# Two-block transformer kernel: adaptive vectors summed in PSUM during the projection, convolutions in a row, expert matrices loaded whole

## The chip, the cores and the metric

The kernel is one program on one core of a Trainium2 chip. The metric is the device time of one execution in microseconds (us). The engines are named as in the profile: PE is TensorE with its matmuls, PEld its weight loads, DVE is VectorE, ACT is ScalarE, POOL is GpSimd, SP is SyncE, which here issues nearly all loads. L180 means line 180 of the kernel before.

## What is computed

One sequence of 1024 tokens with 1024 features goes through two transformer blocks, all in fp32 (fp32 matmuls are done as three fp32r matmuls of a high and a low part). This is the reference's first block, cut to what the change touches:

```
m  = silu(c) @ w_ada + b_ada           # w_ada: 1024 x 6144, split in 6 vectors of 1024
mc = silu(c_ctx) @ w_ada + b_ada       # the same for the context's vector
hx = rms_norm(x,  g) * (1 + m[1]) + m[0]         # 1024 tokens
hc = rms_norm(ctx, g) * (1 + mc[1]) + mc[0]      # 256 tokens
q, k, v, o, gates, ga, gb = split(hx @ w_in + b_in)      # for hc too; w_in: 1024 x 2576
u  = ga * sigmoid(gb)                            # 512 channels
mixer = concat(group_norm(mlstm(q, k, v, gates)) * sigmoid(o),
               silu(layer_norm(conv31(u)))) @ w_out + b_out
x  = x + m[2] * rms_norm(mixer)
h  = rms_norm(x) * (1 + m[4]) + m[3]
x  = x + m[5] * rms_norm(moe(h))                 # 64 experts, 8 per token, and a shared one
```

The mLSTM runs in both directions in chunks of 128 tokens, the two chunks of the context first. `conv31` is a depthwise convolution of width 31 along rows of 64 tokens. Each expert has three matrices of 1 MB (gate and up 1024 x 256, down 256 x 1024). The second block (attention, a state-space layer and 16 experts with the same three matrices) is changed only in the loads of its experts.

## The kernel before

Work on each engine is put in order when the program is built: a list scheduler takes the instructions in program order as priority, plays them on a timeline with estimated costs, and emits one sequence per engine. The exceptions are stretches written out by hand: SP's loads in the input norm (L298 to L306) and in the main loops over the experts. An engine runs its sequence strictly in order. A tile from a pool waits for the last readers of the tile whose room it takes, and so does the load into it.

**Adaptive vectors.** `ada_piece` (L170 to L190) makes 256 of the 6144 columns for both vectors c and c_ctx. It loads 1024 rows x 256 columns (1 MB, in runs of 1 KB) and does eight fp32 matmuls, one for each 128 rows, with `csil` (32 columns, of which two are used) as the stationary operand. The eight go in turn to four column groups of TensorE, so four partial sums stand on 4 x 32 partitions. ACT copies them to `ar` (L182), two matmuls with the selecting matrix `asel` (L187) add the four sums and turn them into a column, and DVE adds the bias into `mcol` (L188). There are 24 pieces. Pieces 0 to 7 (shift and scale of the first norm) are made in `norm_in`, where their loads alternate with those of four tiles of x; the rooms are those of the weight pools `wraw`, `whi`, `wlo`. Pieces 8 to 23 are filler in the mLSTM: `fill` (L230) makes one after each unit, again in `wraw` and `whi` buffers.

**Input norm and projection.** `norm_in` (L252) norms x and then the context: squares on ACT, transposes on PE, scale and shift to a high and a low part. `project` (L320) then makes the parts of w_in one after the other. `weight` loads 1024 x 256 columns into the one `wraw` buffer and splits them (ACT L75, DVE L76). `branch` makes u of 128 channels out of columns of two such loads, `values`, `outgate` and the `feat` loops at the end the rest. `conv` (L392) is 31 DVE operations on 128 channels x 1024 tokens (L398) and then 8 transposes, an ACT copy and a store; conv(0) to conv(2) stand in the projection, conv(3) is called in the mLSTM at unit (4, 1).

**mLSTM.** `mlstm` (L576) first transposes k in 10 steps (PSUM tile `pl`, copied by ACT, L594) and makes the products of q and k in 8 steps (PSUM tile `pi`, copied by ACT, L601), each tile with one buffer. Then come 10 x 2 units (step i, direction d), of which 16 have an output: `D` on ACT (L617) and DVE (L618), matmuls into `pi` and `pn` (L624, L627), `tm` on ACT (L632) and DVE (L633), then the state's update (L669). After it `mix_out` multiplies with w_out.

**Experts.** `weights` (L1123) loads an expert's three matrices by `halves` (L1127): two loads of 512 KB each, 4 KB a partition, into two of eight raw tiles. `split` takes each half apart, high on ACT (L83, `guh` and `wdh`) and low on DVE (L84). Room for `raw` is moved between pools by hand in the set-up (`moe.room`, with Z = 3 extra tiles early on).

Of the kernel before, what the change touches and what calls it, by code (L numbers as in the profile page):

```python
# [29 lines left out]
class Kern:  # L30
# [126 lines left out]
    def ada_setup(self, pool, psp):  # L157
# [7 lines left out]
        self.asel = self.keep.tile([128, 2], F32, name="asel")  # L165
        nc.vector.reduce_sum(self.asel, self.ident.rearrange("p (w q) -> p q w", w=4)[:, 0:2], axis=AX.X)
# [36 lines left out]
    def mixer(self, es0, sec):  # L203
# [14 lines left out]
        with ExitStack() as eh:  # L218
            hx = self.pool(eh, "hx", side="right")
            x = [hx.tile([128, 8, 1024], F32R, name=n) for n in ("hTh", "hTl")]  # L220
            self.wpools(eh, 1, 2, 2)
            psp, ptp = self.pool(eh, "prp", 5, PSUM), self.pool(eh, "prt", 2, PSUM)
            c, raw = self.norm_in(x, eh, pada, ptp, psp, v1.rearrange("p c h e -> p (c h e)"), I['w_in'][0][:, 2064:2320])
            gates, conv = self.project(raw, x, c, kT, qT, v1, gt, pada, psp, ptp, kq, cp)
        sec.bias_prep()
        with ExitStack() as es:
# [19 lines left out]
            for p in todo:  # L246
                fill(9, 1)
# [7 lines left out]
    def norm_in(self, hx, eh, pada, psp, pap, spare, first):  # L255
# [5 lines left out]
        gs = st.tile([128, 2, 8], F32, name="gs")  # L261

# [5 lines left out]
        def rows(xp, xts, g):  # L268
            n = len(xts)
            ss = st.tile([128, 4], F32, name="ss", bufs=2)  # L270
            for t, xt in enumerate(xts):
                scr = xp.tile([128, 1024], BF, name="scr", bufs=1)
                nc.scalar.activation(scr, xt, AF.Square, accum_out=ss[:, t:t + 1])
# [20 lines left out]
        with ExitStack() as es:  # L294
            xp = self.pool(es, "nix")
            xts = []
            finish = lambda: None
            with self.tc.manual_schedule(engines={mybir.EngineType.SP}):  # L298
                for i in range(8):
                    if i < 4:  # L300
                        xts.append(load(xp, I['x'][0], i, 4))
                    last, finish = finish, self.ada_piece(i, st, pap, "pf", ("wraw", "whi", "wlo", "whi", "wlo"))
                    last()
                raw = self.load_w(first)
                xts += [load(spare, I['x'][0], t, 0) for t in range(4, 8)]
            finish()  # L306
            rows(xp, xts[:4], 0)
# [3 lines left out]
            rows(xp, xts[4:], 1)  # L311
# [3 lines left out]
        with ExitStack() as es:  # L315
            xp = self.pool(es, "nic")
            xts = [load(xp, I['ctx'][0], t, 2) for t in range(2)]
            rows(xp, xts, 2)
            columns(xts, 1, hc, 0)
        ew.close()  # L320
        return hc, raw

    def project(self, raw, hx, hc, kT, qT, v1, gt, pada, psp, ptp, kq, cp):
        nc, I = self.nc, self.I
        W, B = I['w_in'][0], I['b_in'][0]
        with ExitStack() as es:
            bp = self.pool(es, "prb")
            self.pcol = self.columns(bp, pada, "pcol", [B[0:512], B[1552:2576], I['conv_b'][0], I['conv_ln_g'][0], I['conv_ln_b'][0],
                                                        I['mlstm_norm_g'][0].rearrange("h p -> (h p)")])
# [48 lines left out]
            us = {}  # L378

            def branch(cc, wb, wa):  # L380
# [4 lines left out]
                for i, s in enumerate(TT):  # L385
                    pb = feat(wb, (cc % 2) * 128, hx, s)
                    sg = cp.tile([128, 512], F32, name="sg", bufs=1)
                    nc.scalar.activation(sg, pb, AF.Sigmoid, bias=bcol[:, 8 + cc:9 + cc])
                    pa = feat(wa, (cc % 2) * 128, hx, s)
# [3 lines left out]
            def conv(cc):  # L393
                u = us[cc]
                y = cp.tile([128, 16, 64], F32, name="y", bufs=1)
# [3 lines left out]
                yf = y.rearrange("p r t -> p (r t)")  # L399
# [28 lines left out]
            wb, wa = self.split_w(raw), self.weight(W[:, 1552:1808])  # L428
            branch(0, wb, wa)
            branch(1, wb, wa)  # L430
# [1758 lines left out]
Z = 3  # L2189
# [72 lines left out]
```

## Time and profile before

| what | value |
|---|---|
| runs, median (lowest to highest) | 2698.14 us (2696.0 to 2704.96), 3 runs |
| profiled execution, its own time | 2692.12 us |
| its span in the profile | 2690.3 us |
| mean granted clock of TensorE | 0.963 |
| busy: PE, PEld, DVE, ACT, POOL | 93%, 79%, 67%, 50%, 20% |
| DMA | 507.52 MB in 259820 packets, mean 189 GB/s |
| queue 1 (SP's loads) | 409.36 MB, 45.4% of 16 engines' span |
| queue 0 (gathers and scatters) | 90.98 MB, 14.9% |

The span is a little shorter than the execution's own time, since that counts what lies around the recorded instructions. Busy shares are means over stages that differ much: start, projection, mLSTM and output product, first experts (about 640 to 1541 us), second block, its experts (from about 2430 us). In a row of the timeline the columns are start, duration, engine, line, operation, output and inputs, their shapes, and the number of instructions; in square brackets stands the idle time ahead of it on its engine and what ended that.

### The profile page before, as it was taken

The numbers are of one execution on the slowest core, as the hardware profiler recorded it, in microseconds if no ns is written. First come the engines' busy times: TensorE is split into PE (matmuls) and PEld (weight loads), VectorE is DVE, ScalarE is ACT, GpSimd is POOL, SyncE is SP. The second block draws the span as 40 slices with busy tenths as digits, with TensorE's granted clock in tenths as the row PEclk, the third lists the DMA queues.
The fourth block names the chain that finished last, engine by engine and source line by source line (L and its number), as shares of the span: only waits on it lengthen the run. The fifth ranks groups of instructions, "written<-read, shape, count | busy, mean of one in ns | idle before, by whom it ended". The sixth has DMA issues, their size and how long they took to land. (4 is left out here: it accounts for less than half of the span.)

```text
span 2690.3 us, 46156 instructions
## 1 busy us (share of the span) xinstructions
PE 2492.9 (93%) x17156; PEld 2127.8 (79%) x17156; DVE 1793.0 (67%) x4037; ACT 1332.8 (50%) x2327; POOL 534.0 (20%) x467
## 2 busy tenths in 40 slices
PE   6999987999999999999999939899999989987996
PEld 4798866987988888888877628688898778976884
DVE  4874788677777788887865453763243876278882
ACT  4322156324677776767765544223222772225773
POOL 0000021311232233233233230230001200002332
PEclk9999998999999999999999969999999999997998
DMA  7111183237899999999999864444311024148995
GB/s 252 33 50 61 44 279 113 103 109 268 244 308 309 312 314 299 307 316 315 301 319 317 252 216 95 123 89 107 114 32 56 1 95 150 56 165 291 320 291 120
DMA packets 259820, 507.52 MB, mean 189 GB/s; under 512 B 68761, under 2 KB 151905, under 8 KB 259592
## 3 DMA queue, kind: packets, MB, share of 16 engines
q1 hardware_dynamic: 231720, 409.36, 45.4%
q0 software_dynamic: 26720, 90.98, 14.9%
q10 hardware_dynamic: 1152, 4.19, 0.4%
q8 instruction: 136, 2.23, 0.3%
q14 instruction: 92, 0.75, 0.1%
HBM read 414.42 MB, written 90.04 MB: 188 GB/s over the span
## 5 line engine op out<-in xcount | busy, mean ns | idle before, releaser
L84 DVE TENSOR_TENSOR gul<-raw,guh 128x1024 fp32r<-128x1024 f32 x288 | 348.4, 1219 | 114.5 <-ACT guh L83 113.4
L83 ACT ACTIVATE guh<-raw 128x1024 fp32r<-128x1024 f32 x288 | 303.1, 1061 | 176.4 <-DMA raw<-in_we_gate_dram 67.8
L1185 PE MATMUL pg<-x,guh 128*128 128x320 f32 (+8 forms) x1248 | 383.7, 371 | 2.6 <-DVE sg L1233 2.6
L1184 PE MATMUL pg<-x,gul 128*128 128x160 f32 (+8 forms) x1092 | 278.1, 256 | 0.0
L1185 PEld LDWEIGHTS pg<-x,guh 128*128 128x128 f32 x1248 | 245.2, 200 | 9.9 <-DVE sg L1233 2.7
L1269 POOL DMA_INDIRECT acc<-y,m1idx x87 | 149.3, 1717 | 492.4 <-DMA acc<-y,m1idx 103.3
L1184 PEld LDWEIGHTS pg<-x,gul 128*128 128x128 f32 x1092 | 219.0, 201 | 3.4 <-issue 0.8
L84 DVE TENSOR_TENSOR wdl<-raw,wdh 128x1024 fp32r<-128x1024 f32 x144 | 175.6, 1222 | 60.9 <-ACT wdh L83 59.3
L88 PE MATMUL psy<-wdh,hh 128*128 128x512 f32 (+8 forms) x444 | 179.2, 405 | 7.4 <-ACT y L1268 7.0
L89 PE MATMUL psy<-wdl,hh 128*128 128x512 f32 (+8 forms) x444 | 175.4, 395 | 0.0
L90 PE MATMUL psy<-wdh,hl 128*128 128x512 f32 (+8 forms) x444 | 169.5, 400 | 0.0
L1097 POOL DMA_INDIRECT xg<-h_d,m1idx x95 | 122.4, 1289 | 180.7 <-PE pt L1119 91.9
L398 DVE SCALAR_TENSOR_TENSOR y<-u,cw,y 128x1024 f32<-128x1024 f32 x120 | 153.9, 1283 | 2.7
L83 ACT ACTIVATE wdh<-raw 128x1024 fp32r<-128x1024 f32 x144 | 151.6, 1054 | 7.3 <-PE psy L90 4.6
L88 PE MATMUL pg<-guh,x 128*112 128x256 f32 (+3 forms) x528 | 152.0, 288 | 1.0 <-ACT x L83 1.0
L1119 PEld LDWEIGHTS pt<-ident,xg 128*128 128x128 f32 (+8 forms) x888 | 119.3, 196 | 40.2 <-issue 18.6
L1119 PE MATMUL pt<-ident,xg 128*128 128x128 f32 (+8 forms) x888 | 134.2, 279 | 17.1 <-DVE x L84 5.3
L89 PE MATMUL pg<-gul,x 128*112 128x256 f32 (+3 forms) x528 | 149.9, 284 | 0.0
L90 PE MATMUL pg<-guh,x 128*112 128x256 f32 (+3 forms) x528 | 149.9, 285 | 0.0
L76 DVE TENSOR_TENSOR wlo<-wraw,whi 128x2048 fp32r<-128x2048 f32 (+2 forms) x37 | 83.3, 2251 | 92.9 <-ACT whi L75 92.8
L89 PE MATMUL pf<-bl,whi 128*128 128x512 f32 (+1 forms) x384 | 140.5, 369 | 3.0 <-DVE bl L1829 2.9
L88 PE MATMUL pf<-bh,whi 128*128 128x512 f32 (+1 forms) x384 | 139.3, 370 | 1.3 <-ACT g L1877 1.3
(906 smaller groups left out, 6972.9 us busy)
## 6 DMA issues: line engine op xcount, KB each, us to landing
raw<-in_we_gate_dram SPq DMA_DIRECT2D x128, 512.0 KB
raw<-in_we_up_dram SPq DMA_DIRECT2D x128, 512.0 KB
raw<-in_we_down_dram SPq DMA_DIRECT2D x128, 512.0 KB
wraw<-in_w_in_dram SPq DMA_DIRECT2D x26, 1024.0 KB
raw<-in_w_e_gate_dram SPq DMA_DIRECT2D x32, 512.0 KB
raw<-in_w_e_up_dram SPq DMA_DIRECT2D x32, 512.0 KB
raw<-in_w_e_down_dram SPq DMA_DIRECT2D x32, 512.0 KB
whi<-in_w_ada_dram SPq DMA_DIRECT2D x14, 1024.0 KB
```

Of the source, the lines that this page charges most:

```text
L76: (eng or nc.vector).tensor_sub(l, raw, h.bitcast(F32))
L83: self.nc.scalar.activation(hi, src, AF.Copy)
L84: self.nc.vector.tensor_sub(lo, src, hi.bitcast(F32))
L88: mm(out, ah, bh, start=first, stop=False)
L89: mm(out, ah, bl, start=False, stop=False)
L90: return mm(out, al, bh, start=False, stop=last)
L398: nc.vector.scalar_tensor_tensor(y, u[:, :, j:j + 64], cw[:, cc, j:j + 1], y, op0=OP.mult, op1=OP.add)
L1097: self.k.nc.gpsimd.indirect_dma_start(out=xg[:n], out_offset=None, in_=self.h_d[:, :], in_offset=bass.IndirectOffsetOnAxis(ap=idx[:n], axi ...
L1119: nc.tensor.transpose(pt[:, i, :n], xg[:n, 4 * j + i::8], k.ident[:n, :n])
L1184: mm(ps[:, 0], wl[:, q], x[:, i, 0, :m], start=False, stop=False)
L1185: mm(ps, wh[:, q], x[:, i, :, :m], start=i == 0, stop=i == 7)
L1269: nc.gpsimd.indirect_dma_start(out=self.acc_d[:, :], out_offset=bass.IndirectOffsetOnAxis(ap=idx[:n, b:b + 1], axis=0), in_=y[:n], in_offs ...
```

## The change

1. `ada_piece` now takes 128 rows and 2048 columns (group 0, runs of 8 KB) or 1024 columns (groups 1 and 2, half pieces, runs of 4 KB) and does four matmuls, one for each column group of TensorE. The sum over the 1024 rows is made in one PSUM bank over the group's 8 or 16 pieces. `ada_finish` closes a group: one ACT copy, four transposes, one or two adds on DVE. `asel` is gone. The bank comes from a pool of its own, `pra`; the projection's pool `prp` has 4 banks instead of 5.
2. The 32 half pieces of groups 1 and 2 are made in `project`, in eight calls of `ada(4)`, and load into a pool `wada` with one buffer of 512 KB. The mLSTM has none any more.
3. The projection's order is new. Weights of a branch are loaded as the 128 + 128 columns of one channel chunk (`pair`, two loads with runs of 512 bytes). The context's norm is a function, called after the third `ada(4)`, and `pcol` is loaded in `norm_in`. conv(0) to conv(3) all stand in the projection; their transposes and stores are `convout`, and only convout(3) is left for the mLSTM, at unit (2, 1).
4. In the mLSTM's set-up the PSUM tiles take turns over `pl` and the two of `pd`, and over `pi` and `pn`. The second tile of `kt` and the gates' scratch get other rooms.
5. `halves` loads a whole matrix in one load of 1 MB (8 KB a partition) into one raw tile and returns its two halves; the 8 raw tiles of 4 KB a partition become 4 of 8 KB, with Z = 1. The shared expert's raw tiles are paired in the same way.

The diff, cut to its core (the new rooms of the gates' scratch and the places of the expert stage's hand-over are left out):

```
-    def ada_piece(self, i, sp, psp, tag, slots):
+    def ada_piece(self, g, i, ps, raw, h, parts):
 
 
         nc = self.nc
-        name = slots[i % len(slots)]
-        pool = getattr(self, name)
-        raw = pool.tile([128, 8, 256], F32, name=name)
-        nc.sync.dma_start(raw, self.I['w_ada'][0][:, i * 256:(i + 1) * 256].rearrange("(c p) n -> p c n", p=128))
-        ps = psp.tile([128, 512], F32, name=tag)
-        for k in range(8):
-            w = slice(32 * (k % 4), 32 * (k % 4) + 32)
-            nc.tensor.matmul(ps[w, :256], self.csil[:, k], raw[:, k], start=k < 4, stop=k >= 4)
-        r = sp.tile([128, 256], F32, name="ar", bufs=2)
-        nc.scalar.activation(r, ps[:, :256], AF.Copy)
-
-        def finish():
-            pt = psp.tile([128, 512], F32, name=tag)
-            for j in range(2):
-                nc.tensor.matmul(pt[:, 2 * j:2 * j + 2], r[:, j * 128:(j + 1) * 128], self.asel, start=True, stop=True)
-            nc.vector.tensor_tensor(self.mcol[:, 2 * i:2 * i + 2], pt[:, :4].rearrange("p (a b) -> p a b", a=2),
-                                    self.acol[:, 16 + 2 * i:18 + 2 * i][:, :, None].to_broadcast([128, 2, 2]), op=OP.add)
-        return finish
+        n = 2048 // parts
+        q, o = n // 4, g * 2048 + h * n
+        nc.sync.dma_start(raw, self.I['w_ada'][0][i * 128:(i + 1) * 128, o:o + n])
+        for j in range(4):
+            nc.tensor.matmul(ps[32 * j:32 * j + 32, h * q:h * q + q], self.csil[:, i], raw[:, j * q:(j + 1) * q], start=i == 0 and h == 0,
+                             stop=i == 7 and h == parts - 1)
+
+    def ada_finish(self, g, ps, r, psp, tag, parts):
+
+        nc = self.nc
+        nc.scalar.activation(r, ps, AF.Copy)
+        pt = psp.tile([128, 512], F32, name=tag)
+        for i in range(4):
+            nc.tensor.transpose(pt[:, i * 128:(i + 1) * 128], r[:, i * 128:(i + 1) * 128], self.ident)
+        m = 4 // parts
+        for h in range(parts):
+            c = slice(16 * g + 4 * m * h, 16 * g + 4 * m * h + 4 * m)
+            nc.vector.tensor_tensor(self.mcol[:, c].rearrange("p (j i) v -> p j i v", i=m),
+                                    pt[:, 128 * m * h:128 * m * h + 128 * m].rearrange("p (i j q) -> p j i q", i=m, j=4)[:, :, :, 0:2],
+                                    self.acol[:, 16:64][:, c].rearrange("p (j i) -> p j i", i=m)[:, :, :, None].to_broadcast([128, 4, m, 2]), op=OP.add)
...
-            psp, ptp = self.pool(eh, "prp", 5, PSUM), self.pool(eh, "prt", 2, PSUM)
-            c, raw = self.norm_in(x, eh, pada, ptp, psp, v1.rearrange("p c h e -> p (c h e)"), I['w_in'][0][:, 2064:2320])
-            gates, conv = self.project(raw, x, c, kT, qT, v1, gt, pada, psp, ptp, kq, cp)
+            psp, ptp = self.pool(eh, "prp", 4, PSUM), self.pool(eh, "prt", 2, PSUM)
+            psa = self.pool(eh, "pra", 1, PSUM)
+            c, context, raw = self.norm_in(x, eh, pada, ptp, psa, v1.rearrange("p c h e -> p (c h e)"), kT.rearrange("p f t -> p (f t)"),
+                                           [I['w_in'][0][:, 2064:2192], I['w_in'][0][:, 1552:1680]])
+            gates, convout = self.project(raw, x, c, context, kT, qT, v1, gt, pada, psp, ptp, psa, kq, cp)
...
-            todo = iter(range(8, 24))
             squares = ob.tile([128, 8, 4], F32, name="ss")
 
             def fill(i, d):
-                p = next(todo, None)
-                if p is not None:
-                    self.ada_piece(p, cp, pada, "pada", ("wraw", "whi", "whi"))()
-                if (i, d) == (4, 1):
-                    conv(3)
+                if (i, d) == (2, 1):
+                    convout(3)
...
-            finish = lambda: None
+            scr = xp.tile([128, 1024], BF, name="scr")
+            ps = psa.tile([128, 512], F32, name="pa")
             with self.tc.manual_schedule(engines={mybir.EngineType.SP}):
                 for i in range(8):
                     if i < 4:
                         xts.append(load(xp, I['x'][0], i, 4))
-                    last, finish = finish, self.ada_piece(i, st, pap, "pf", ("wraw", "whi", "wlo", "whi", "wlo"))
-                    last()
-                raw = self.load_w(first)
+                    n = ("wraw", "whi", "wlo", "whi", "wlo")[i % 5]
+                    self.ada_piece(0, i, ps, getattr(self, n).tile([128, 2048], F32, name=n), 0, 1)
+                raw = self.load_w(*first)
                 xts += [load(spare, I['x'][0], t, 0) for t in range(4, 8)]
-            finish()
-            rows(xp, xts[:4], 0)
+                self.pcol = self.columns(st, pada, "pcol", [B[0:512], B[1552:2576], I['conv_b'][0], I['conv_ln_g'][0], I['conv_ln_b'][0],
+                                                            I['mlstm_norm_g'][0].rearrange("h p -> (h p)")])
+            self.ada_finish(0, ps, st.tile([128, 512], F32, name="mtmp", bufs=2), psp, "pt", 1)
...
+        def context():
+            xts = [load(spare2, I['ctx'][0], t, 0) for t in range(2)]
+            rows(spare2.bitcast(BF)[:, 4096:5120], xts, 2)
             columns(xts, 1, hc, 0)
-        ew.close()
-        return hc, raw
-
-    def project(self, raw, hx, hc, kT, qT, v1, gt, pada, psp, ptp, kq, cp):
+            ew.close()
+        return hc, context, raw
...
+            us, ys = {}, {}
+            pieces = iter([(g, i, h) for g in (1, 2) for i in range(8) for h in range(2)])
+            wa = self.pool(es, "wada")
+
+            def ada(n):
+                for _ in range(n):
+                    g, i, h = next(pieces)
+                    if not i and not h:
+                        self.apart = psa.tile([128, 512], F32, name="pa")
+                    self.ada_piece(g, i, self.apart, wa.tile([128, 1024], F32, name="wada"), h, 2)
+                    if i == 7 and h:
+                        self.ada_finish(g, self.apart, wa.tile([128, 1024], F32, name="wada")[:, :512], ptp, "pt", 2)
+
+            def branch(cc, w):
...
+            pair = lambda cc: self.split_w(self.load_w(W[:, 2064 + 128 * cc:2192 + 128 * cc], W[:, 1552 + 128 * cc:1680 + 128 * cc]))
+            w = self.split_w(raw)
+            ada(4)
+            branch(0, w)
+            ada(4)
+            w = pair(1)
+            branch(1, w)
+            ada(4)
             w0 = self.weight(W[:, 512:768])
+            context()
+            conv(0)
             w1 = self.split_w(self.load_w(W[:, 768:1024], W[:, 1536:1552]))
-            conv(0)
             values(0, w0)
+            ada(4)
+            convout(0)
+            w = pair(2)
+            values(1, w1)
+            ada(4)
+            with ExitStack() as e1:
+                gates = self.mlstm_gates(gt, kq, qT.rearrange("p f t -> p (f t)"), self.pool(e1, "mlt"), ptp)
             w0 = self.weight(W[:, 1024:1280])
-            values(1, w1)
+            branch(2, w)
+            ada(4)
+            conv(1)
+            w = pair(3)
+            outgate(0, w0)
+            ada(4)
+            convout(1)
             w1 = self.weight(W[:, 1280:1536])
-            gates = self.mlstm_gates(gt, kq, self.pool(es, "mlt"), ptp)
-            conv(1)
-            outgate(0, w0)
-            wb = self.weight(W[:, 2320:2576])
+            branch(3, w)
+            ada(4)
+            conv(2)
+            w = self.weight(W[:, 256:512])
             outgate(1, w1)
-            wa = self.weight(W[:, 1808:2064])
-            branch(2, wb, wa)
-            branch(3, wb, wa)
-            w, w1 = self.weight(W[:, 256:512]), self.weight(W[:, 0:256])
-            conv(2)
+            convout(2)
+            w1 = self.weight(W[:, 0:256])
+            conv(3)
...
-                pk = psp.tile([128, 512], F32, name="pl")
+                pk = psp.tile([128, 512], F32, name=("pl", "pd", "pd")[c % 3], bufs=1 + (c % 3 > 0))
...
-                pk = psp.tile([128, 2, 4, 128], F32, name="pi")
+                pk = psp.tile([128, 2, 4, 128], F32, name=("pi", "pn")[c % 2])
...
-            moe.pools(self.pool(es1, "m1r"), raw=8)
+            moe.pools(self.pool(es1, "m1r"), raw=4)
...
     def halves(self, src):
+
         kc = src.shape[1]
-        out = []
-        for j in range(2):
-            raw = self.tile("raw", [128, kc // 2, 2048 // kc], F32)
-            self.k.nc.sync.dma_start(raw, src[:, j * kc // 2:(j + 1) * kc // 2])
-            out.append(raw)
-        return out
+        raw = self.tile("raw", [128, 8, 256], F32).rearrange("p a b -> p (a b)").rearrange("p (c n) -> p c n", c=kc)
+        self.k.nc.sync.dma_start(raw, src)
+        return [raw[:, j * kc // 2:(j + 1) * kc // 2] for j in range(2)]
...
-Z = 3
+Z = 1
```

## Rows read from the trace of the kernel before

**Rows 1.** The stretches of the span; PE clock granted, DMA share, GB/s at the end

```profile
core 0: us, PE busy (x) PEld busy (x) DVE busy (x) ACT busy (x) POOL busy (x), PEclk, DMA share, GB/s
0.00:45.00 45.00, 25.36 (x169) 14.13 (x169) 11.09 (x42) 13.08 (x24) 1.67 (x10) 1.00 0.91 306
...
93.00:334.00 241.00, 240.75 (x1448) 208.95 (x1449) 165.55 (x193) 55.32 (x90) 7.01 (x11) 0.99 0.17 51
334.00:450.00 116.00, 93.22 (x969) 69.70 (x967) 101.67 (x238) 74.85 (x238) 22.54 (x24) 0.90 0.67 214
...
640.00:1000.00 360.00, 352.70 (x2398) 315.56 (x2397) 276.17 (x552) 249.14 (x394) 102.46 (x71) 0.99 0.97 298
1000.00:1541.00 541.00, 530.12 (x3791) 439.34 (x3790) 398.40 (x846) 370.38 (x617) 169.39 (x113) 0.99 0.99 307
```

**Rows 2.** The waits between 640 and 1541 us: total, times, longest

```profile
ACT guh L83 <- DMA raw<-in_we_gate_dram: 66.2, 37, 4.9
...
PEld psy L88 <- ACT y L1268: 6.5, 8, 1.5
...
SPq L1132 <- DVE gul L84: 171.6, 106, 11.2
```

**Rows 3.** Short stretches, columns as in rows 1

```profile
20.00:34.00 14.00, 11.65 (x79) 6.59 (x71) 4.97 (x19) 2.54 (x6) 0.00 (x0) 1.00 1.09 341
37.00:43.00 6.00, 3.74 (x25) 2.38 (x25) 1.08 (x3) 2.70 (x3) 0.00 (x0) 1.00 1.05 403
1299.00:1303.00 4.00, 4.00 (x33) 4.00 (x33) 2.62 (x6) 2.13 (x6) 2.56 (x2) 1.00 1.02 412
81.00:93.00 12.00, 7.33 (x38) 5.45 (x37) 7.53 (x24) 6.67 (x14) 0.95 (x6) 0.85 0.01 3
434.00:444.00 10.00, 4.18 (x20) 3.48 (x20) 9.90 (x34) 8.88 (x35) 1.19 (x1) 0.51 0.07 13
```

**Rows 4.** The timeline at the end of the start

```profile
42.12 0.37 ACT L182 ACTIVATE ar<-pf 128x256 f32<-128x256 f32 x1
...
44.64 0.24 DVE L309 SCALAR_TENSOR_TENSOR gs<-mcol,acol 128x8 f32<-128x8 f32 x2
```

**Rows 5.** PE's timeline in the mLSTM, one piece among other matmuls

```profile
396.34 0.22 PE L613 MATMUL pd<-maskn,identb 128*128 128x128 bf16 x1
396.40 0.22 PE L612 MATMUL pd<-M,sel 96*128 96x128 bf16 x1
396.55 1.07 PE L180 MATMUL pada<-wraw,csil 128*32 128x256 f32 x16
397.55 0.66 PE L663 MATMUL pl<-v,kw 128*64 128x129 f32 x8
...
399.43 0.56 PE L187 MATMUL pada<-asel,ar 128*128 128x2 f32 x4
```

**Rows 6.** The timeline of one 1 MB load and its first use

```profile
281.24 0.38 SPq L67 DMA_DIRECT2D wraw<-in_w_in_dram  x1
...
286.61 1.92 ACT L75 ACTIVATE whi<-wraw 128x2048 fp32r<-128x2048 f32 x1 [7.16 <-DMA wraw<-in_w_in_dram]
```

**Rows 7.** Groups on DVE, 334 to 450 us: busy, mean ns, idle before

```profile
L398 DVE SCALAR_TENSOR_TENSOR y<-u,cw,y 128x1024 f32<-128x1024 f32 x23 | 29.8, 1296 | 0.4
```

**Rows 8.** Groups on ACT, 334 to 450 us

```profile
L617 ACT ACTIVATE D<-pd,cq 128x128 f32<-128x128 f32 x64 | 18.4, 371 | 6.7 <-PE pn L627 6.7
...
L182 ACT ACTIVATE ar<-pada 128x256 f32<-128x256 f32 x16 | 6.2, 389 | 15.5 <-PE pada L180 15.5
```

**Rows 9.** The timeline of the mLSTM, marks on DVE and ACT

```profile
365.48 0.68 DVE L633 TENSOR_TENSOR tm<-pn,tm 128x516 f32<-128x516 f32 x1
...
392.76 0.70 DVE L633 TENSOR_TENSOR tm<-pn,tm 128x516 f32<-128x516 f32 x1 [0.34 <-ACT tm L632]
...
409.16 1.91 ACT L75 ACTIVATE whi<-wraw 128x2048 fp32r<-128x2048 f32 x1 [4.42 <-DMA wraw<-in_w_out_dram]
...
443.52 0.68 DVE L633 TENSOR_TENSOR tm<-pn,tm 128x516 f32<-128x516 f32 x1
```

More of the change, by code (lines that the diff above doesn't have):

```diff
@@ L245, in mixer @@
             self.mlstm(kT, qT, v1, gates, hm, fill, done)
-            for p in todo:
-                fill(9, 1)
             ek.close()
@@ L253, in mixer, with norm_in @@
             self.mix_out(hm, em, ob, squares)
-    def norm_in(self, hx, eh, pada, psp, pap, spare, first):
+    def norm_in(self, hx, eh, pada, psp, psa, spare, spare2, first):
         nc, I = self.nc, self.I
@@ L261, in norm_in @@
         gs = st.tile([128, 2, 8], F32, name="gs")
+        B = I['b_in'][0]
         def load(xp, src, t, bufs):
@@ L266, in load, with rows @@
             return xt
-        def rows(xp, xts, g):
+        def rows(scr, xts, g):
             n = len(xts)
@@ L310, in norm_in @@
             columns(xts[:4], 0, hx, 0)
-            rows(xp, xts[4:], 1)
+            rows(scr, xts[4:], 1)
             columns(xts[4:], 0, hx, 512)
@@ L314, in norm_in, with project @@
         hc = [hp.tile([128, 8, 256], F32R, name=n) for n in ("hCh", "hCl")]
[L315 to L318, printed above, removed]
+        def context():
+            xts = [load(spare2, I['ctx'][0], t, 0) for t in range(2)]
+            rows(spare2.bitcast(BF)[:, 4096:5120], xts, 2)
             columns(xts, 1, hc, 0)
-        ew.close()
-        return hc, raw
-    def project(self, raw, hx, hc, kT, qT, v1, gt, pada, psp, ptp, kq, cp):
+            ew.close()
+        return hc, context, raw
+    def project(self, raw, hx, hc, context, kT, qT, v1, gt, pada, psp, ptp, psa, kq, cp):
         nc, I = self.nc, self.I
@@ L394, in conv @@
                 u = us[cc]
-                y = cp.tile([128, 16, 64], F32, name="y", bufs=1)
+                y = ys[cc] = cp.tile([128, 16, 64], F32, name="y", bufs=1)
                 nc.vector.tensor_scalar(y, u[:, :, 0:64], cw[:, cc, 0:1], cb[:, cc:cc + 1], op0=OP.mult, op1=OP.add)
@@ L398, in conv, with convout @@
                     nc.vector.scalar_tensor_tensor(y, u[:, :, j:j + 64], cw[:, cc, j:j + 1], y, op0=OP.mult, op1=OP.add)
-                yf = y.rearrange("p r t -> p (r t)")
+            def convout(cc):
+                yf = ys[cc].rearrange("p r t -> p (r t)")
                 for g in range(2):
@@ L455, in project, with mlstm_gates @@
                     nc.scalar.activation(qT[:, f, s], ps, AF.Identity, bias=bcol[:, f:f + 1])
-            return gates, conv
-    def mlstm_gates(self, gt, gp, tp, psp):
+            return gates, convout
+    def mlstm_gates(self, gt, gp, room, tp, psp):
         nc = self.nc
@@ L462, in mlstm_gates @@
         R = 104
-        U = tp.tile([128, 2, 128], F32, name="U")
+        U = room[:, 0:256].rearrange("p (a b) -> p a b", a=2)
         pool.memset(U, 0.0)
@@ L476, in mlstm_gates @@
         tr(pu[:R, 128:256], U[:, 1, :R], self.ident)
-        t = lambda n: tp.tile([R, 128], F32, name=n)
+        names = ("li", "gx", "gab", "lf", "gz", "gw2", "gpl", "gb", "gh", "gcm")
+        t = lambda n: room[:R, 256 + 128 * names.index(n):384 + 128 * names.index(n)]
         li, x, ab, lf = t("li"), t("gx"), t("gab"), t("lf")
@@ L519, in mlstm_gates @@
         dve.tensor_tensor_scan(fl(mr), fl(sb[:, 0]), fl(sb[:, 1]), 0.0, op0=OP.add, op1=OP.max)
-        rb = tp.tile([1, 3, 128], F32, name="rb")
+        rb = room[:1, 1536:1920].rearrange("p (a b) -> p a b", a=3)
         pool.memset(rb, 0.0)
@@ L582, in mlstm @@
         with ExitStack() as es:
-            gp = self.pool(es, "mlg")
             wp = self.pool(es, "mlw", 2)
@@ L586, in mlstm @@
             kq = lambda c: kqs[c // 4][:, c % 4]
-            kts = [self.wlo.tile([128, 8, 4, 64], F32, name="wlo"), gp.tile([128, 2, 4, 64], F32, name="kt")]
+            kts = [self.wlo.tile([128, n, 4, 64], F32, name="wlo") for n in (8, 2)]
             kt = lambda c: kts[c // 8][:, c % 8]
@@ L876, in moe1 @@
                     moe.pools(self.pool(e1, "m1z"), raw=Z)
-                    moe.room['raw'] = raw[:4] + raw[8:] + raw[4:8]
+                    moe.room['raw'] = raw[:2] + raw[4:] + raw[2:4]
                     moe.start()
                     moe.split(0, 0)
-                    moe.room['raw'] = raw[:8]
+                    moe.room['raw'] = raw[:4]
                 fill(16)
@@ L888, in moe1 @@
                 moe.main()
-                head([moe.tile("raw", [128, 4, 256], F32).rearrange("p a b -> p (a b)") for _ in range(7)], moe.pst)
+                places = [moe.tile("raw", [128, 8, 256], F32).rearrange("p a b -> p (a b)") for _ in range(4)]
+                head([v[:, j:j + 1024] for v in places for j in (0, 1024)][:7], moe.pst)
             raw[:] = [(mc, 2, "gu" + n) for n in "hl"]
@@ L1288, in shared_up @@
         for f in range(2):
-            for w in (wg, wu):
-                raw.append(part(self.tile("raw", [128, 4, 256], F32)))
+            both = self.tile("raw", [128, 8, 256], F32)
+            for j, w in enumerate((wg, wu)):
+                raw.append(part(both[:, 4 * j:4 * j + 4]))
                 nc.sync.dma_start(raw[-1], w[:, f * 128:f * 128 + 128].rearrange("(c p) n -> p c n", p=128))
@@ L2180, in experts @@
             em.close()
-            moe.pools(k.pool(es, "m2w"), raw=8, gu=6, wd=3, x=2, xg=4, oh=2, q=2, sg=2, su=2, hh=2, hl=2, y=3)
+            moe.pools(k.pool(es, "m2w"), raw=4, gu=6, wd=3, x=2, xg=4, oh=2, q=2, sg=2, su=2, hh=2, hl=2, y=3)
             with moe.ordered():
```

15 lines of the change are left out of this document (3 added, 12 removed).

## The prediction, made before the changed kernel ran

> **What bounds the kernel now.** The page comes first: TensorE is busy 93% of the span, and the chain of waits is mostly PE. That share is a mean over stages, so the second view is the table of stretches [rows 1]. It shows three kinds of stage. Before 45 us the DMA engines are the limit (share 0.91, PE 25 of 45 us). From 93 to 334 us, the projection, PE is busy 240.75 of 241 us: any matmul put there lengthens the kernel by its own time. From 334 to 450 us, the mLSTM scan, nobody is full (PE 93, DVE 102, ACT 75 of 116 us): it is bound by hand-overs. In moe1 (640 to 1541 us) PE and DMA are both nearly full: PE has 7.3 + 10.9 = 18.2 us of idle time in 901 us while the DMA share is 0.97 to 0.99. The third view is the waits of moe1 [rows 2]: ACT waits 66.2 us on gate matrices, in 37 waits, but PE's weight load shows only 6.5 us behind ACT, so little of that arrives.
>
> The profiled execution took 2692.12 us (span 2690.3). The median of the runs is 2698.14 us, 6.0 us more. I sum against 2692.1 and put the sum on the median.
>
> **Start: -8 us (bounds 0 and -9).** The adaptive vectors' first third, 8 pieces of 1 MB, arrives before x can be modulated. While its 1 KB runs load, DMA moves 341 GB/s; while x loads in 4 KB runs it moves 403 [rows 3]. The front transfers w_ada 8.39 MB and 2.1 MB of x, about 10.5 MB: at 341 that is 30.8 us, at 403 to 412 it is 25.5 to 26. The new runs are 8 KB; I take the 4 KB rate, which gives -5. The other part is behind the last load: the last piece's copy `ar` runs only at 42.12, behind ACT's split of w_in, and `gs` is made at 44.64 [rows 4]. After the change the last piece is four matmuls, one copy, four transposes and one add, some 3 us instead of 6 after the last load. Together -8. Zero would come if w_in and x, still queued behind, set the time anyway; -9 if 8 KB runs are faster still.
>
> **45 to 93 us: -3 (bounds +4 and -5).** The context's norm and columns and the bias columns' wait leave this stretch; between 81 and 93 us PE was busy 7.33 of 12 us [rows 3], so 4.7 us can go. But only one channel pair's weights are loaded early now, so an early wait on the second pair can give some back. The context's 16 transposes and DVE work come back under the projection's matmuls, whose DVE was 165.6 of 241 us.
>
> **Projection: +22 for work, +4 for waits.** It takes in 32 half pieces of four 128x32 matmuls over 256 columns. The old piece, eight such matmuls, stands among matmuls of another shape: these follow each other at 0.06 us (396.34, 396.40), the piece begins 0.15 after the last of them and the next shape starts at 397.55 [rows 5]. From 396.46 that is 1.09 us, with 0.09 of it a change of shape; I count a change at each end, 0.2. A half piece is then (1.09 - 0.2)/2 + 0.2 = 0.65 us, and 32 of them 20.8. Two finishes, four transposes each and a copy off PE, add some 0.5 each. That is +22. The bounds are 32 x 0.45 = 14 (no price for shape) and 32 x 1.09 = 35 (nothing saved by halving).
>
> The half pieces load through one buffer, so a load of 512 KB starts only when the piece before has been multiplied. A 1 MB load that nothing held back was issued at 281.24 and used at 286.61 [rows 6], 5.4 us; less 0.52 MB at 412 GB/s (1.27 us) a half takes 4.1 us. The projection has 263/32 = 8.2 us of PE work per piece, so the loads fit if the order spreads them. PE runs in order: a piece placed too early holds all matmuls behind it. I take +4 in all; below zero is excluded, since PE has no idle time here, and rival A is the upper end.
>
> DVE gets conv(3) as well, 31 operations of 1.296 [rows 7], 40 us in all, of which 30 were in the scan: 165.6 + 30 + the context's few still leaves DVE under 220 of about 265 us. If that cover were gone, conv(3) would run on into the scan and some of the gain below would be lost. SP has 32 more issues of under 0.4 us and DMA share was 0.17 [rows 1]: both free. The loads that move past each other on SP's queue are weights due tens of us later.
>
> **Scan, 334 to 450 us: -28 (bounds -10 and -40).** What leaves, from [rows 5, 7, 8]: on DVE 23 conv operations, 29.8 us, and 16 small adds; on PE 16 pieces of 1.09 plus their selecting matmuls of 0.56, 26 us; on ACT 16 copies, 6.2, and 15.5 us in which ACT idled for them. So DVE falls to 70, PE to 67, ACT to 69 of 116 us. The scan is a chain through all three, so it doesn't fall to 70. I read it in three parts [rows 9]. (i) The set-up runs from 334 to the first `tm` of 365.48; its 18 copies to `kt` and `kq` each wait on a single PSUM bank. With two or three banks in turn PE and ACT overlap, and no pieces and conv operations stand between: -10, then -4 as the first units start freely. (ii) 365 to 393 holds seven units, 3.9 us each; without piece and conv I take 3.2: -5. (iii) From 393 to 443.5, another 50 us, ACT stood 4.42 us on w_out's load, which was queued behind ada loads in the same pool; that goes, and the same 0.7 us per unit over seven units: -9. Together -28. What is late next is ACT: `D` alone takes 18.4 us and `tm` has as many copies. The clock is the limit to trust: in 434 to 444 us the granted clock was 0.51 with PE busy 4.18 of 10 [rows 3]; where PE becomes sparser this may spread, which is rival D.
>
> **Whole matrices: moe1 0, moe2 +1.** A matrix comes in one load of 128 runs of 8 KB instead of two with 4 KB. Raw room is the same 4 MB, but it is given back in units of 1 MB, and the first split now waits for a whole matrix. The half loads flow at 412 GB/s already [rows 3], so I see no gap to close, and PE is the limit: 0. Bounds are rivals B and C. moe2 is alike with fewer matrices: +1.
>
> Sum: -8 - 3 + 22 + 4 - 28 + 0 + 1 = -12, so 2680 for a profiled execution and 2698 - 12 = 2686 us for the median. My forecast's own range is 2670 to 2702.
>
> **Rivals.**
> A, slower: PE waits for `wada`. The mechanism is the single buffer at PE's place in the order: if each piece comes 1.27 us early (the transfer of a half alone), 32 x 1.27 = 41 us instead of 4, so 2686 + 37 = 2723. It decides from 16 us, 0.5 per piece, where the gain is gone. For it: PE is in order, full, and has nothing else once it waits. Against: 8.2 us per piece, twice the load's time, and PE idled only 0.25 us in the whole projection so far [rows 1], weights loaded ahead.
>
> B: whole loads cost moe1. ACT's first split waits 1.27 us longer in the 37 waits of [rows 2], 47 us; of the 66.2 us it waits now at most 18.2 reached PE, 0.27 of it, so 47 x 0.27 = +13: 2699. For it: ACT's waits are on the gate matrix, the first one of each expert. Against: loads run ahead, SP itself stood 171.6 us waiting for room.
>
> C: moe1 is DMA-bound and gains. From 1 KB runs at 341 to 4 KB at 412 GB/s a straight line (0.69 ns a run, 2.31 a KB) gives 427 at 8 KB, 3.5% of 901 us, 32 us if all were weights; PE's idle time caps it at 18: 2668. For it: DMA share 0.97 to 0.99. Against: PE at 0.98 as well.
> A rule stands beside C: the Trainium skill, page "DMA: Bandwidth & Descriptors", section "Bandwidth", asks for DMAs of at least 1 MiB. By its fit (section on the anatomy of one DMA, for loads issued from GpSimd) each avoided load would spare a fixed 2.0 us, an estimate of 384 us over 192 matrices; 412 GB/s in a row of half-size loads contradicts that as a cost in throughput, so C keeps the price from the rows.
>
> D: the scan stays bound by ACT and the clock and gains 10, not 28: 2704. For it: granted clock 0.51, ACT at 8.88 and DVE at 9.90 of 10 us there. Against: the idle time of ACT is named, and is waits for pieces.
>
> **Chances.** Forecast 0.48, A 0.16, B 0.12, C 0.12, D 0.12. What can be told from no change is 0.3%, 8 us: below 2690 is faster, above 2706 slower. Faster: 0.32 of the forecast, nearly all of C, little of B: 0.46. Slower: nearly all of A, half of D, a quarter of B and a rest: 0.24. Same 0.30. The range 2660 to 2724 runs from just beyond C to A.
>
> **What would show it.** Start: `gs` near 36.5 instead of 44.64. Projection: PE's wait before the pieces under 4 us in all, each piece near 0.65. No conv operation after 340 and the scan under 95 us long. In moe1 unchanged length, PE idle still near 18 us. I am wrong if PE shows waits of over 0.5 us per piece on `wada`, if the scan's units stay at 3.9 us, or if moe1's length moves by more than 8 us.

## The result and the profile after: 1.1% slower

The changed kernel takes 2722.78 us (median of 4 runs, 2717.09 to 2741.6) against 2697.07 us of the kernel before (4 runs, 2693.08 to 2704.96). The ratio is 1.0111, 95% interval 1.0074 to 1.0149: 26 us slower, where 12 us faster was forecast. The profiled execution took 2717.09 us. This is the head of its page:

```profile
span 2715.3 us, 44663 instructions
...
PE 2487.8 (92%) x17008; PEld 2110.4 (78%) x17008; DVE 1790.6 (66%) x4017; ACT 1315.2 (48%) x2304; POOL 538.2 (20%) x467
```

All engines are busy for about as long as before, on a span 25 us longer. So no work was added on balance: the time went into waits. The table of stretches shows where; it has the columns of [rows 1], with a cut at the changed kernel's own borders of the scan:

```profile
core 0: us, PE busy (x) PEld busy (x) DVE busy (x) ACT busy (x) POOL busy (x), PEclk, DMA share, GB/s
...
351.00:435.00 84.00, 64.88 (x625) 53.09 (x623) 67.93 (x175) 60.98 (x203) 23.37 (x24) 0.86 0.23 76
640.00:1000.00 360.00, 353.36 (x2432) 316.67 (x2430) 275.39 (x556) 246.58 (x394) 102.09 (x69) 1.00 0.94 298
1000.00:1541.00 541.00, 517.52 (x3656) 425.89 (x3655) 388.06 (x818) 357.72 (x600) 168.04 (x110) 0.98 0.93 298
```

Against [rows 1]: the projection ends at 351 instead of 334, and the scan after it takes 83 us instead of 109. The transposes that make the router's logits on PE, before and now, are:

```profile
590.73 0.71 PE L821 MATMUL pt<-ident,rwT 64*128 64x64 f32 x8
```

```profile
586.21 0.71 PE L848 MATMUL pt<-ident,rwT 64*128 64x64 f32 x8
```

So at the logits the new kernel is still 4.5 us ahead. Then come the experts. From the last of these transposes to the last gate matmul of the first experts it was 591.2 to 1524.9, 933.7 us; it is 586.7 to 1542.5, 955.8 us. In the row from 1000 us PE is busy 517.52 us instead of 530.12 and the DMA share is 0.93 instead of 0.99. The loss of 22 us in this stage is most of what there is; in this one execution some 3 us more are lost in the second block's experts and some 4 after the last matmul. The 3 us appear in the run with half loads below as well, so they are not the whole loads'. The waits in this stage, which answer to [rows 2] (total, times, longest), are ACT's on the gate matrix, PE's weight loads behind ACT, and SP's for room:

```profile
ACT guh L83 <- DMA raw<-in_we_gate_dram: 96.9, 36, 6.5
```

```profile
PEld psy L88 <- ACT y L1294: 11.8, 5, 6.9
...
PEld psy L88 <- ACT hh L83: 7.1, 8, 2.1
```

```profile
SPq L1159 <- DVE gul L84: 180.2, 49, 8.3
```

ACT waits 96.9 us on gate matrices instead of 66.2, in about as many waits, and PE's weight loads stand behind ACT's `y` and `hh` for 18.9 us instead of 6.9, of which 6.5 behind `y`. One piece of the timeline shows how the two hang together (start, duration, engine; in brackets the idle time ahead and its releaser):

```profile
1227.28 1.22 DVE L84 TENSOR_TENSOR gul<-raw,guh 128x1024 fp32r<-128x1024 f32 x1
...
1228.53 0.33 SPq L1159 DMA_DIRECT2D raw<-in_we_gate_dram  x1
...
1236.54 2.00 ACT L83 ACTIVATE guh<-raw 128x1024 fp32r<-128x1024 f32 x2 [4.28 <-DMA raw<-in_we_gate_dram]
1238.44 0.67 ACT L1294 ACTIVATE y<-psy,m1wsl 128x512 f32<-128x512 f32 x1
...
1239.16 0.43 PE L88 MATMUL psy<-wdh,hh 128*48 128x512 f32 x1 [2.63 <-ACT y L1294]
```

DVE ends the second `gul` of a matrix at 1228.50 and only then is its 1 MB free: SP issues the next gate load at 1228.53. ACT uses it at 1236.54, after 4.28 us of idle time. Behind that split on ACT stand the `y` copies of the unit before, which empty PSUM: PE's next down product starts at 1239.16, 2.63 us late.

### The profile page after: what moved, and what is told of

The parts are those of the page before. It is cut to its first block, busy times and chain, and to the rows that moved or that the text cites. A ratio compares the mean times of both kernels' runs of the same rounds, so it can differ in the third digit from the quotient of the medians.

```text
span 2715.3 us, 44663 instructions
## 1 busy us (share of the span) xinstructions
PE 2487.8 (92%) x17008; PEld 2110.4 (78%) x17008; DVE 1790.6 (66%) x4017; ACT 1315.2 (48%) x2304; POOL 538.2 (20%) x467
## 5 line engine op out<-in xcount | busy, mean ns | idle before, releaser
L83 ACT ACTIVATE guh<-raw 128x1024 fp32r<-128x1024 f32 x288 | 291.9, 1055 | 157.6 <-DMA raw<-in_we_gate_dram 98.8
L1295 POOL DMA_INDIRECT acc<-y,m1idx x87 | 156.1, 1795 | 522.9 <-ACT guh L83 103.8
L1294 ACT ACTIVATE y<-psy,m1wsl 128x512 f32<-128x512 f32 (+8 forms) x174 | 116.6, 680 | 59.4 <-DMA acc<-y,m1idx 25.0
L76 DVE TENSOR_TENSOR wlo<-wraw,whi 128x2048 fp32r<-128x2048 f32 (+2 forms) x37 | 83.3, 2251 | 91.5 <-ACT whi L75 91.3
```

The lines of the kernel that those rows point to most:

```text
L83: self.nc.scalar.activation(hi, src, AF.Copy)
L1294: nc.scalar.activation(y[:n, q], ps[:n], AF.Copy, scale=w[:n, b:b + 1])
L1295: nc.gpsimd.indirect_dma_start(out=self.acc_d[:, :], out_offset=bass.IndirectOffsetOnAxis(ap=idx[:n, b:b + 1], axis=0), in_=y[:n], in_offs ...
```

## The experiments

All times are medians, against 2694.99 to 2699.7 us of the kernel before on the same chip.

**Undoing the whole loads.** The two loads and the half tiles of before, eight of them and Z = 3, with everything else as changed:

```
-        raw = self.tile("raw", [128, 8, 256], F32)...
-        self.k.nc.sync.dma_start(raw, src)
+        for j in range(2):
+            raw = self.tile("raw", [128, kc // 2, 2048 // kc], F32)
+            self.k.nc.sync.dma_start(raw, src[:, j * kc // 2:(j + 1) * kc // 2])
...
-            moe.pools(self.pool(es1, "m1r"), raw=4)
+            moe.pools(self.pool(es1, "m1r"), raw=8)
```

> The changed kernel with only the whole-matrix loads undone: each expert matrix comes again in two loads of 512 KB into two of eight raw tiles. Theory R (the loss is made by the whole loads, since raw room is given back 1 MB at a time and queue 1 runs dry): the time between 640 and 1541 us falls by about 24 us, the gain of the front stays, 2693 us (2688 to 2698), DMA share in 1100 to 1500 us back at 0.97 to 1.01. Rival P (the loss is made by the new order of the front, which delays or shifts everything behind it): stays near 2720.

Measured: 2686.01 us, ratio 0.995 (0.9931 to 0.9969). The loss goes, a little further than expected, and the experts' stage is 928.0 us long. The other four parts of the change are worth 13.7 us against the kernel before. That this is close to the 12 forecast for the whole, and the median equal to the forecast's 2686, is luck: at the logits the traced execution is only 3.9 us ahead of the kernel before, where 13 were forecast, and where the other 10 us of the median come from is not shown.

> The kernel before with only the whole-matrix loads added. Theory R: slower by the same amount, 2697 + 25 = 2722 us (2715 to 2730), nothing changed before 640 us. Rival P: 2697, within 8 us.

The whole loads alone, put on the kernel before: 2723.18 us, ratio 1.0104 (1.0072 to 1.0137), stage 960 us. Both runs say the same: the whole loads cost 24 us on one side and 37 on the other. In the experts' stage alone it is 26 and 28 us, so the front has no part in it. The stage itself varies between executions: the five traces with eight half tiles (the kernel before and the runs that keep them) have 928 to 939 us, the three with four whole tiles in one load each 953 to 960.

**What of the whole load costs.** Loads in two halves, but into one tile of 1 MB:

```
+        raw = self.tile("raw", [128, 8, 256], F32)...
+        out = [raw[:, j * kc // 2:(j + 1) * kc // 2] for j in range(2)]
+        for j in range(2):
+            self.k.nc.sync.dma_start(out[j], src[:, j * kc // 2:(j + 1) * kc // 2])
```

> The changed kernel, raw tiles of 1 MB, but each filled by two loads of 512 KB with runs of 4 KB, each split waiting for its own half. Theory R (room given back in 1 MB units): the loss stays, 2715 to 2723 us, SP still waits for whole tiles. Rival A (the first split waits for a whole matrix to arrive, 1.27 us more each time): the loss goes, 2693 us. Rival K (8 KB packets hold up gathers and scatters): the loss goes as well, and POOL's waits for its own DMAs fall.

Measured: 2750.17 us, ratio 1.0203 (1.0169 to 1.0238); the stage is 987 us long in the traced execution, which took 2763.38. The loads, their order and their 4 KB runs are those of the run with half loads. The split of a half needs only its own half, as two splits of one gate matrix show, each waiting for its load:

```profile
1210.61 1.06 ACT L83 ACTIVATE guh<-raw 128x1024 fp32r<-128x1024 f32 x1 [5.86 <-DMA raw<-in_we_gate_dram]
1212.31 1.06 ACT L83 ACTIVATE guh<-raw 128x1024 fp32r<-128x1024 f32 x1 [0.64 <-DMA raw<-in_we_gate_dram]
```

What differs is that the room comes back in units of 1 MB, and that costs 64 us; theory R had the direction and not the size, and why it is so much was not followed up. It also shows what the single load is worth: with the same tiles it is 27 us faster than two. The stretch from 1100 to 1500 us (columns of [rows 1]) of the kernel before, the changed one, the half loads and this one, in this order:

```profile
1100.00:1500.00 400.00, 394.21 (x2853) 326.95 (x2851) 298.22 (x651) 273.56 (x459) 128.23 (x87) 0.99 0.99 311
```

```profile
1100.00:1500.00 400.00, 379.37 (x2705) 307.78 (x2704) 283.38 (x630) 257.25 (x434) 126.28 (x84) 0.97 0.92 296
```

```profile
1100.00:1500.00 400.00, 397.82 (x2905) 327.65 (x2906) 301.55 (x659) 278.11 (x467) 129.04 (x89) 1.00 0.99 315
```

```profile
1100.00:1500.00 400.00, 376.51 (x2643) 312.43 (x2642) 284.44 (x618) 255.62 (x428) 123.65 (x80) 0.97 0.93 286
```

The DMA share falls from 0.99 to 0.92 and 0.93, although the changed kernel's loads are no dearer, and PE falls with it. What a byte costs stands in the view of the queues (packets, MB, share of 16 engines' time) of the same stretch, again changed kernel, half loads, two loads into a whole tile:

```profile
q1 hardware_dynamic: 12453, 90.66, 62.2%
```

```profile
q1 hardware_dynamic: 26658, 97.07, 67.2%
```

```profile
q1 hardware_dynamic: 23845, 86.85, 64.4%
```

62.2% of 400 us for 90.66 MB is 2.74 us a MB in 8 KB packets; the half loads pay 2.77 and the last run 2.97. Against the half loads the longer runs are cheaper by 1%, less than the price moves between kernels with the same runs: with eight half tiles it is 2.77 to 2.83 in the five traces. The Trainium skill, page "DMA: Bandwidth & Descriptors", section "Bandwidth", asks for DMAs of at least 1 MiB. Here that rule agrees with the price among equal tiles (2.74 against 2.97), and against half tiles it buys 1%, not clear of that spread, and loses the room.

**More and less room.** Seven half tiles instead of eight (`raw=7`), nine, and five whole tiles, for which one of two one-hot tiles was given up as well. The ninth and the fifth tile stand in a pool of their own; their room comes from constants that are no longer kept after the mLSTM:

> As the run with half loads, but seven raw tiles of 512 KB instead of eight, 3.5 MB of room. Theory R: a 1 MB tile with one half split is half idle, so four of them work like about seven half tiles: this one loses some 10 to 25 us against the run with half loads, 2703 to 2718 us. Rivals A and K: no change against half loads, 2693 us.

Measured: 2729.15 us, 43 us slower than with eight, where 10 to 25 were expected. All seven come from one pool, so this run is the test of room as an amount.

> The run with half loads and a ninth raw tile of 512 KB in the main stage of the first experts (its room comes from three constants that are no longer kept after the mLSTM). Theory R (room for loads ahead is what the experts' stage lives on; seven tiles cost 43 us more than eight): faster than eight, by 5 to 20 us, 2666 to 2681 us. Rival S (eight tiles saturate the DMA engines, share 0.99; more room buys nothing): 2686 within 5 us.

Measured: 2720.01 us, ratio 1.0078 (1.0058 to 1.0098). Both theories missed: with one more tile it is 34 us slower.

> The changed kernel with whole loads and a fifth raw tile of 1 MB in the main stage of the first experts; to make room one of two one-hot tiles is given up. Theory R: the loss against half loads goes, 2680 to 2695 us, DMA share of 1100 to 1500 us back at 0.97 or more. Rival L (a split waits for the whole matrix to arrive, whatever the room): stays near 2722 us.

Measured: 2756.98 us, ratio 1.021 (1.0188 to 1.0232). It too is slower than with four, but it gave up the one-hot tile too, so it says less. Below are, of the run with nine tiles, its stretch, SP's largest wait between 640 and 1541 us and, for comparison, the same wait with eight tiles (total, times, longest), then its loads on SP's timeline:

```profile
1100.00:1500.00 400.00, 385.06 (x2750) 315.33 (x2749) 291.53 (x639) 263.52 (x444) 122.46 (x84) 0.99 0.93 303
```

```profile
SPq L1164 <- DVE wdl L81: 270.2, 50, 24.9
```

```profile
SPq L1159 <- DVE wdl L84: 138.3, 70, 8.9
```

```profile
1216.84 2.46 SPq L1164 DMA_DIRECT2D raw<-in_we_gate_dram  x2
1232.92 0.88 SPq L1164 DMA_DIRECT2D raw<-in_we_up_dram  x2
1233.99 0.89 SPq L1164 DMA_DIRECT2D raw<-in_we_down_dram  x2
1235.67 1.40 SPq L1164 DMA_DIRECT2D raw<-in_we_gate_dram  x2
1237.32 1.08 SPq L1164 DMA_DIRECT2D raw<-in_we_up_dram  x2
```

SP stands from 1219.3 to 1232.92 on `wdl`, the split of an earlier down matrix, then issues eight half loads in 5.5 us. The cause is how the ninth tile was added. The program gives it out by turn, to every ninth load, whether another tile is free or not, and that turn falls, once in three experts, on the first half of an up matrix, while the tile still holds the second half of the down matrix two experts back, the last split of its expert. Between 650 and 1500 us this load comes up 19 times and is issued over 6 us behind the load before it 18 times; of all other loads only 11 are. SP works in order, so the loads behind it wait too, though other tiles are free, and then come in a burst. So this run did not test more room by itself: theory R stays untested on that side, and which tile a load has to wait for counts as well as how many there are.

With eight tiles the picture is another one. In the kernel before 325 of 356 loads between 650 and 1500 us, and in the run with half loads 332 of 362, were issued within 0.06 us of the end of a split on DVE, one load behind each split; with the four whole tiles of the changed kernel it is 164 of 176, with nine half tiles 181 of 343 (all counted in the traces). One such pair in the kernel before:

```profile
1118.62 1.21 DVE L84 TENSOR_TENSOR wdl<-raw,wdh 128x1024 fp32r<-128x1024 f32 x1
```

```profile
1119.86 0.33 SPq L1132 DMA_DIRECT2D raw<-in_we_gate_dram  x1
```

**Whether the order of the splits does it.** The split of the down matrix called ahead of the down product:

```
+            self.split(i + 1, 2)
             if i:
                 r1, j1, m1, b1 = U[i - 1]
...
-            self.split(i + 1, 2)
```

> The changed kernel (four whole tiles), with one line moved: the split of the next expert's down matrix is called ahead of this unit's down product instead of behind it, so that it ranks before the y copies. Theory O (the tiles are given back by splits that stand late in ACT's and DVE's order; with whole tiles every late split holds 1 MB): faster than the changed kernel by 8 to 25 us, 2698 to 2715 us, and the loads of up and down are issued earlier before their first split than 9.9 and 15.4 us. Rival R (room alone): 2722 within 6 us.

> Nine half tiles with the same line moved. With nine tiles the loads of the up matrix wait for the tiles of an earlier down matrix (SP stood 258 us on DVE's wdl). Theory O: most of the loss against eight halves goes, 2680 to 2700 us, and SP's wait on wdl falls by more than half. Rival: the ninth tile's loss has another cause, 2720 within 6 us.

> Eight half tiles (the run at 2686 us) with the same line moved, as the control. Theory O: the order of before fits eight halves, so little to win: 2680 to 2692 us. If any change of the order costs here (the fast kernels all share one order of ACT, DVE and PE in this stage), it is slower, 2700 us or more, and the loss of the whole loads may be one of order as such.

Measured: four whole tiles 2725.37 us (1.0116, 1.0094 to 1.0139), nine halves 2727.1 (1.0118, 1.0101 to 1.0135), eight halves 2693.73 (0.9985, 0.9965 to 1.0004). The line recovers nothing, though it does change the order: with four whole tiles SP's wait on `wdl` between 640 and 1500 us falls from 119.6 to 105.6. With nine half tiles that wait is 266.6 us after 257.9. The theory that these splits rank too late falls, as far as this one line goes. The control, too, is no better: 0.15% under the kernel before, where it had been 0.5% without the line.

**The set-up of the scan alone**, on the kernel before: only the two `name=` lines with the PSUM tiles in turn.

> The kernel before with only the PSUM tiles of the mLSTM's set-up taking turns. The prediction's step (single banks hold the set-up): the first tm comes up to 10 us after the projection's end sooner, the total falls by 5 to 10 us. Rival: the pieces and the convolution that stand between still hold ACT and DVE, the total moves by less than 3 us.

Measured: 2697.37 us, ratio 0.9994 (0.9979 to 1.0009): nothing. Yet its trace has the whole gain of the scan: first and last `tm` on DVE, then PE's work, and last the start of the output product in the kernel before:

```profile
355.10 0.68 DVE L633 TENSOR_TENSOR tm<-pn,tm 128x516 f32<-128x516 f32 x1
...
417.27 0.69 DVE L633 TENSOR_TENSOR tm<-pn,tm 128x516 f32<-128x516 f32 x1
...
428.13 1.94 PE L180 MATMUL pada<-wraw,csil 128*32 128x256 f32 x16 [2.27 <-DVE mcol L188]
...
448.43 0.58 PE L88 MATMUL py<-whi,hh 128*128 128x256 f32 x1 [2.51 <-ACT hh L731]
```

```profile
450.38 0.39 PE L88 MATMUL py<-whi,hh 128*128 128x256 f32 x1 [1.55 <-ACT hh L731]
```

The first `tm` comes at 355.10 instead of 365.48 and the last at 417.27 instead of 443.52 [rows 9], 26 us earlier. Then the last five pieces of w_ada, filler of the scan, stand alone from 417 to 444 us and take longer (1.94 us instead of 1.07 [rows 5], at a granted clock of 0.55 between 417 and 450 us), and the output product starts at 448.43 instead of 450.38. The gain was given back to what had been hidden. So the turns in PSUM are worth nothing while the pieces stay; the pieces elsewhere without the turns were not run.

**The start's loads.** In the changed kernel SP issued loads that nobody needed yet ahead of the last pieces of w_ada:

```profile
9.34 0.24 SPq L368 DMA_DIRECT2D y<-in_conv_w_dram  x1
10.60 0.83 SPq L173 DMA_DIRECT2D wada<-in_w_ada_dram  x1
13.10 1.61 SPq L262 DMA_DIRECT2D kT<-in_ctx_dram  x2
16.92 0.33 SPq L173 DMA_DIRECT2D wraw<-in_w_ada_dram  x1
...
20.67 0.33 SPq L173 DMA_DIRECT2D wlo<-in_w_ada_dram  x1
...
38.35 0.60 ACT L181 ACTIVATE mtmp<-pa 128x512 f32<-128x512 f32 x1 [18.99 <-PE pa L175]
...
39.92 0.17 DVE L308 SCALAR_TENSOR_TENSOR gs<-mcol,acol 128x8 f32<-128x8 f32 x1
```

```
+            with self.tc.issue_after(self.hold):       # the load of x's last tile
                 ada(4)
...
+            with self.tc.issue_after(self.hold):
+                xts = [load(spare2, I['ctx'][0], t, 0) for t in range(2)]
```

> The run with half loads, and the loads of the context and of the first wada pieces queued behind the loads of x on SP, so that 1.5 MB no longer go ahead of the last three pieces of w_ada. The prediction's step (the start is set by bytes through the DMA engines): 1.5 MB at 360 to 419 GB/s, gs 3.7 to 4.4 us earlier, at about 36 instead of 40.2, and the total 2 to 4 us lower. Rival: the context and the pieces arrive late and PE stands for them in 50 to 98 us, total the same or up to 4 us higher.

Measured, on half loads: 2672.42 us, ratio 0.9906 (0.9884 to 0.9928). This is the fastest of all versions, 26 us under the kernel before and 50 under the changed one. `gs` comes 3.5 us earlier than with half loads alone (40.08), close to what was expected:

```profile
36.58 0.24 DVE L308 SCALAR_TENSOR_TENSOR gs<-mcol,acol 128x8 f32<-128x8 f32 x2
```

The logits are reached at 579.2 instead of 587.3, 8 us earlier. The total falls by 14 us against the run with half loads, where 2 to 4 were expected: the start explains 3.5, the stretch between it and the logits 4.6, and the rest was not followed up.

## Why the prediction was wrong, step by step

**Whole matrices: moe1 0. This step failed**, and with it the sign. The prediction said: "Raw room is the same 4 MB, but it is given back in units of 1 MB", and then took "no gap to close, and PE is the limit: 0". The size of that half sentence was never worked out. Measured: 22 us in the stage, 24 to 37 us by taking the loads out or putting them in. "PE is the limit" left out that the DMA engines, at a share of 0.97 to 0.99, had no slack either: with loads issued later their share from 1100 to 1500 us fell to 0.92, and PE's busy time with it, from 394 to 379 us. SP's 171.6 us of waiting for room [rows 2] were read as "loads run ahead". The loads did not run ahead: 325 of 356 were issued right behind the split that freed room, so the splits set their pace.

Rival B had the place right and ACT's wait as the messenger, at +13; its mechanism, the arrival of the second half, is not needed for the loss: with two loads into a whole tile each split waits for its own half and the time is still worse. What it adds in the changed kernel was not measured apart. Rival C's gain from a longer run was small (2.77 to 2.74 us a MB, 1%, where 3.5% was worked out) and is outweighed. Rival A gave 2723, nearly the measured time, by a mechanism that didn't occur. PE's wait on `wada` over the projection (total, times, longest) is:

```profile
PE pa L175 <- DMA wada<-in_w_ada_dram: 1.4, 2, 0.8
```

**Start, -8:** `gs` at 39.92 instead of 44.64, -4.7. The step behind the last load came out (matmuls to `gs` in under 3 us). The bytes were miscounted: the loads of `wada`, context and conv_w that SP put ahead, 1.6 MB, were not in the sum. Held back, the 1.5 MB of `wada` and context give 3.5 us.

**45 to 93 and projection, -3 + 22 + 4 = +23:** from `gs` to the projection's end it was 289.6 us and is 311.2, +21.7: the sum is right. A half piece in the projection, among its matmuls (128x256 at a pitch of 0.12):

```profile
128.79 0.28 PE L90 MATMUL pf<-whi,hTl 128*128 128x256 f32 x1
129.00 0.64 PE L175 MATMUL pa<-wada,csil 128*32 128x256 f32 x8
129.57 0.38 PE L88 MATMUL pf<-whi,hTh 128*128 128x256 f32 x1
```

From 128.91 to 129.57 and 0.1 behind it (the next matmul follows at 129.79, 0.22 on), 0.76 us, for 0.65 predicted: over 32 pieces 3.5 us too few. The waits that were set at 4 us are 1.4, so the two errors nearly cancel.

**Scan, -28:** from the end of the projection to the last `tm` it was 109.3 us and is 83.3, -26. The sum is right, by luck: its parts were not what the runs show.

```profile
351.15 0.69 ACT L482 ACTIVATE qT<-pf,pcol 128x512 f32<-128x512 f32 x1 [4.91 <-PE pf L90]
...
372.53 0.66 DVE L660 TENSOR_TENSOR tm<-pn,tm 128x516 f32<-128x516 f32 x1
...
434.41 0.70 DVE L660 TENSOR_TENSOR tm<-pn,tm 128x516 f32<-128x516 f32 x1
```

```profile
410.00:435.00 25.00, 18.03 (x100) 14.96 (x97) 20.58 (x52) 18.18 (x77) 6.27 (x5) 0.53 0.12 42
434.60:473.00 38.40, 32.40 (x243) 30.76 (x244) 32.50 (x107) 23.14 (x50) 0.28 (x1) 0.85 0.29 90
```

The set-up is 21 us instead of 31, the 10 forecast for the banks. From the first to the last `tm` it is 62 us instead of 78, and the forecast gave that to the pieces and convolution operations that leave. But the kernel before with the turns alone has the same 62 us (355.10 to 417.27) with eight of the 16 pieces and some convolution operations still between, and 83.3 us for the whole scan. So that the pieces' leaving shortens the units is not shown; why the turns do is open. The two stretches show the clock: 0.53 granted in the scan's last 25 us, 0.85 in the 38 us behind the last `tm`. In the same 38 us the kernel before had 0.94, after a scan in which PE had the pieces to do. What was not seen is that output product: from the last `tm` to the logits it was 147.7 us and is 152.3, 4.6 us given back. Whether the clock alone did that was not tried. So the front gave 4.5 us where 13 were forecast: 3.3 missing at the start, 1.9 in the scan and 4.6 here, less 1.3 in the projection.

## What to carry to other kernels

The size of a tile is also the size in which its room comes back, and a merged load needs the larger tile. Where loads wait for room and the DMA engines are nearly full, halving the number of loads by doubling the tiles cost about as much here as taking one of eight tiles away (37 and 43 us). Before merging loads, read what the load queue waits for, and whether each load is issued right behind the end of the work that frees its room. A tile that is added by a fixed turn can hold up all the loads behind it. And a gain in a stage counts only if the filler that was hidden in it has moved out as well.

## What the runs showed of the hardware

In the experts' stage a run of 8 KB was hardly cheaper than one of 4 KB: 2.74 us a MB in the changed kernel against 2.77 with half loads and 2.83 in the kernel before. At the start, from 5 to 20 us, loads in 8 KB and 4 KB runs moved 419 GB/s in the changed kernel, where 1 KB and 4 KB runs moved 368 in the kernel before and 341 from 20 to 34 us [rows 3].
